# Stick-breaking weights as differences, and the softmax division and the sum of product halves moved to the gates

## Chip, core and metric

The program runs on one core of a Trainium2 chip. The metric is the device time of one execution in microseconds (us). The core's engines are TensorE (PE, with its weight loads listed as PEld), VectorE (DVE), ScalarE (ACT), GpSimd (POOL) and SyncE (SP). In this kernel SP issues every DMA.

## The reference, cut to what matters

One layer of a hybrid encoder, for a prompt of 1024 frames and a sample of 32 frames with shared weights. All is float32. The features are 1024; `w_in` gives eight groups of 512 columns, and A and B have 8 heads of 64 each.

```python
u = rmsnorm(h, g_pre) @ w_in
qa, ka, va, ga, qb, kb, vb, gb = split(u)

# A: band attention
s = einsum('bqhd,bkhd->bhqk', q, k) * SCALE + bias_table[:, clip(k_pos - q_pos)]
oa = softmax(where(ok, s, -1e30)) @ v        # 640 keys at most for each 128 queries

# B: stick breaking, k_pos < q_pos
z = einsum('bqhd,bkhd->bhqk', q, k) * SCALE
log_1m = where(causal, log_sigmoid(-z), 0)
after = cumsum(log_1m, reverse=True) - log_1m
ob = where(causal, exp(log_sigmoid(z) + after), 0) @ v

y = concat(oa * silu(ga), ob * silu(gb)) @ w_out
h = h + rmsnorm(y, g_post)
h = h + sigmoid(h @ w_ple_gate) * (p @ w_ple)
```

The sigmoid products of B are a running product from the right: with s' = sigmoid(-z) and C(k) the product of s' over the keys from k on, the weight of key k is sigmoid(z_k) · C(k+1), which equals C(k+1) − C(k), since sigmoid(z) = 1 − sigmoid(−z).

## The kernel before, in words

**Accuracy and matmuls.** Every float32 product is made of three matmuls with operands split in a high and a low part (`wh`, `wl`, `hnh`, `hnl`, `wTh`, `wTl`). A projection chunk is 352 columns (3 chunks cover the 1056 frames) and takes 24 matmuls.

**Stages.** First x is normalised, turned and split (to about 60 us of the profiled span), while the first weights come in. Then attention runs for four pairs of heads of A and four of B, in turn (A0, B0, A1, B1 and so on), woven with the projections q, k and v of the next pair (60 to 480 us). The last pair, B3, is woven with the eight gate products gA0 to gB3 (482 to 606). Then come the product of p with `w_ple`, and the output projection and gate as Strassen-like block products (to about 797 us).

**Attention.** `attention` (L778) makes three kinds of units for each head. `scores(i)` (L813) makes the scores of query block i (128 queries) in PSUM tiles `SA` or `SB`, and the weights from them in two SBUF tiles, `om` and `be` (the names of the two rings, L514). For A, DVE adds the bias and takes the maximum, negates it, ACT makes the exponential with its sum, DVE takes the reciprocal, POOL multiplies. For B, DVE adds the mask, ACT makes two sigmoids, of −s in `om` and of s in `be`; DVE scans the products over `om` from the right, and POOL multiplies `be` by it. `weights_t(i)` (L860) turns the weights: PE transposes into PSUM `ptw`, ACT copies the high part to `wTh`, DVE subtracts for the low part `wTl`. For A's blocks 4 and 6 (`ROUND`, L31) it goes another way, here called the swap path: DVE transposes in squares of 32, one DMA writes them to DRAM (`swapA`), four DMAs read them back turned into `be`, ACT casts `wTh` and DVE subtracts `wTl`. `values(g)` (L910) multiplies four query blocks by the value operand (`v2`), into a PSUM tile `PV` of 128 partitions, whose two halves of 64 belong to high and low parts of the values. ACT copies one half, DVE adds the other, and a DMA stores 64 rows in `o_dr`.

**Gates.** In `col_steps` (L712) a gate chunk of 352 columns gets its `o_dr` part by a DMA that is issued with its first matmuls (tiles `ogg`, at L730). At its end ACT makes a sigmoid, DVE multiplies the sum by it, POOL multiplies by `ogg`, and a DMA stores to `og_dr` (tiles `sgg`, L741 to L746).

**What sets the order.** All calls are recorded (`Recorder.add`, L308, so that L450 stands for every line in the profile) and `order()` (L372) writes a fixed order for each engine. It is a list scheduler: it gives each operation a cost and the time at which its inputs are there, and among the ready ones takes attention first on PE and the earliest recorded on other engines. Its times carry margins ahead of PE (400 ns) and behind a DMA (2000 ns). In this order each engine runs strictly. In the built program each DMA on SP waits, besides its own inputs, until the DMA eight places before it has landed.

**At the start** SP loads the norm's weights, p, x's tiles 0 to 2, the first weights of k and q, x's tile 3, then masks, tiles 5 and 6, `wr_vA` in two halves around tile 4, and tile 7. x's tiles are `om` in the profile, but tiles 3 and 4, `x`. For each tile ACT squares it with a sum (`be<-om`), POOL makes `rs`, DVE scales it to `be`, PE turns it (`ptx`) and ACT and DVE split it (`hnh`, `hnl`). POOL splits the weights `wr` of k, q and v in between; those of vA go to the tile `wTl`.

Of the kernel before, what the change touches and what calls it, by code (L numbers as in the profile page):

```python
# [8 lines left out]
F32 = mybir.dt.float32  # L9
# [21 lines left out]
ROUND = {"A": ((4,),(6,)), "B": ()}  # L31
# [127 lines left out]
class Segments:  # L159


    def __init__(self, buf, start, step, n):
        self.buf, self.start, self.step, self.n = buf, start, step, n
        self.shape = [buf.shape[0], n, P]
        self.box = (buf.box[0], (start, start + (n - 1) * step + P))

    def get(self):
        base = self.buf.get()[:, self.start:self.start + P]
        return bass.AP(tensor=base.tensor, offset=base.offset, ap=[base.ap[0], [self.step, self.n], [1, P]])
# [83 lines left out]

class Engine:
# [9 lines left out]
class Recorder:  # L264
# [43 lines left out]
    def add(self, eng, what, args, kw):  # L308
        writes, reads = [], []
        method = what[1] if isinstance(what, tuple) else ""  # L310
        for i, a in enumerate(args):
            if isinstance(a, (View, Raw, Segments)):
                (writes if i == 0 or (method == "tensor_tensor_reduce" and i == 7) else reads).append(a)
        for k, a in kw.items():
            if isinstance(a, (View, Raw, Segments)):
                (writes if k in ("out", "accum_out") else reads).append(a)
        o = self.node(eng, what, args, kw, set())
        for mine, write in ((reads, False), (writes, True)):
            for v in mine:
                b = v.buf  # L320
                hit = False
                for other, box, wrote in b.uses:
                    if other is not o and (write or wrote) and all(p < y and x < q for (p, q), (x, y) in zip(v.box, box)):
# [6 lines left out]
                b.uses.append((o, v.box, write))  # L330
        o.busy, o.late = self.cost(eng, method, args, kw, writes, reads)
        o.shared = eng == "POOL"
        if eng == "DVE":
            sbuf = [v for v in reads if isinstance(v, (View, Segments)) and not v.buf.psum and v.free() > 4]
# [3 lines left out]
    def cost(eng, method, args, kw, writes, reads):  # L338
# [3 lines left out]
        psum = any(isinstance(v, (View, Segments)) and v.buf.psum for v in reads)  # L342
# [97 lines left out]
    def emit(self, tc):  # L440
        ops = self.order()
        with tc.manual_schedule():
            for o in ops:
# [3 lines left out]
                args = [a.get() if isinstance(a, (View, Raw, Segments)) else a for a in o.args]  # L447
                kw = {k: a.get() if isinstance(a, (View, Raw, Segments)) else a for k, a in o.kw.items()}
# [7 lines left out]
def stream_step(  # L456
# [22 lines left out]
    o_dr = [scratch([P, T], f"o_dr{n}") for n in range(8)]  # L479
# [34 lines left out]
    ring0, ring1 = Arena(rec, at, "om", 3076), Arena(rec, at, "be", 3384)  # L514
    ringh, ringl = (Arena(rec, at, x, 33 * P, F32R) for x in ("wTh", "wTl"))
# [10 lines left out]
    NAMES = ["qA", "kA", "vA", "gA", "qB", "kB", "vB", "gB"]  # L526

# [14 lines left out]
    def ensure(j):  # L542
# [6 lines left out]
        if j == 2:  # L549
            pair = [ringl.tile([P, 2, 4, P], f"w{x}_{kind}{p}") for x in "hl"]  # L550
# [14 lines left out]
    def load_x(t):  # L565
        n = min(P, T - t * P)
        if t == 3:
            x34.append(at.tile([P, ringh.cols], F32, tag="wTh", name="x34")[:, 0:2 * D].rearrange("p (a c) -> p a c", a=2))
# [37 lines left out]
    def bias_rows():  # L606

        rb = ring0.tile([8, 257], "rb")
        dma(rb, rel_bias[0])
        R = ring1.tile([8, 768], "R")  # L610
# [101 lines left out]
    def col_steps(j):  # L712
# [7 lines left out]
        def mms(c, part):  # L720
# [9 lines left out]
            if k == "g" and part == 0:  # L730
                box["og"] = at2.tile([P, CH], F32, tag="bias", name=f"og{kind}{p}_{c}", bufs=2)
                dma(box["og"], o_dr[n][:, cs])
# [8 lines left out]
            if k == "g":  # L741
# [3 lines left out]
                nc.gpsimd.tensor_tensor(sg, sg, box["og"], ALU.mult)  # L745
                dma(og_dr[n, :, cs], sg)  # L746
            elif k == "q":
                nc.scalar.activation(box["st"][:, cs], acc, AF.Copy, scale=SCALE)
# [28 lines left out]

    def attention(ab, p, h):  # L778
# [5 lines left out]
        def begin():  # L784
            if ab == "A":
                bias = at2.tile([P, 640], F32, tag="bias", name=f"bias{nm}", bufs=2)
                dma(bias, bias_src(2 * p + h, P, 0, 640))
                nc.gpsimd.memset(bias[0:HD, 0:HD], NEG)
                nc.gpsimd.memset(bias[HD:P, 576:640], NEG)
# [4 lines left out]

        together = {i: g for g in ROUND[ab] for i in g}
        whole, done_with = {}, []
# [4 lines left out]
        def rooms(i):  # L801

            more = ab == "B"
            g = together.get(i, (i,))
            if g not in whole:
                n = sum(cost(x) for x in g) * P
                whole[g] = ring0.tile([P, n + more * len(g)], f"om{nm}_{i}"), ring1.tile([P, n], f"be{nm}_{i}")
            k, n = g.index(i), cost(i) * P
            a = sum(cost(x) for x in g[:k]) * P
            w0, w1 = whole[g]  # L810
            return w0[:, a + more * k:a + more * k + n + more], w1[:, a:a + n]

        def scores(i):  # L813
# [5 lines left out]
            w0, w1 = rooms(i)  # L819
# [8 lines left out]
            if ab == "B":  # L828
# [3 lines left out]
                nc.gpsimd.memset(w0[:, n:n + 1], 1.0)  # L832
                for a, b, s in pieces:
                    nc.scalar.activation(w0[:, a:b], s, AF.Sigmoid, scale=-1.0)
                for a, b, s in pieces:
                    nc.scalar.activation(w1[:, a:b], s, AF.Sigmoid)
                for a, b, s in reversed(pieces):
                    rev = w0[:, a + 1:b + 1][:, ::-1]
                    nc.vector.tensor_tensor_scan(rev, rev, s, 1.0 if b == n else w0[:, b + 1:b + 2], ALU.mult, ALU.bypass)
                nc.gpsimd.tensor_tensor(w1[:, 0:n], w1[:, 0:n], w0[:, 1:n + 1], ALU.mult)  # L840
            else:
                m = small.tile([P, 4], F32, tag="stat", name=f"stat{nm}_{i}", bufs=6)
                for j, (a, b, s) in enumerate(pieces):
                    nc.vector.tensor_tensor_reduce(
                        w0[:, a:b], s, box["bias"][:, n - b:n - a][:, ::-1], 1.0,
                        -3e38 if j == 0 else m[:, j - 1:j], ALU.add, ALU.max, m[:, j:j + 1])
# [7 lines left out]
        wT = {}  # L854
# [5 lines left out]
        def weights_t(i):  # L860
            g = i // 4
            step, size = LAID[ab, g]
            if g not in wT:
                wT[g] = [x.tile([P, size * P], f"{x.name}{nm}_{g}") for x in (ringh, ringl)]
            b0 = lo_block(i)
            w0, w1 = state.pop(i)
            n = i + 1 - b0
            at_ = ((i - 4 * g) * step + b0) * P
            hi, lo = (x[:, at_:at_ + n * P] for x in wT[g])
            if i in together:  # L870

                group = together[i]
                done_with.append((i, hi, lo))
                if i != group[-1]:
                    return
                w0, w1 = whole[group]
                m = sum(cost(x) for x in group)
                first = {x: sum(cost(y) for y in group[:k]) for k, x in enumerate(group)}
                squares = w0[:, 0:m * P].rearrange("p (c b q) -> p b c q", c=4, q=32)
                for x, _, _ in done_with:  # L880
                    y = slice(first[x], first[x] + cost(x))
                    nc.vector.transpose(squares[:, y], w1[:, y.start * P:y.stop * P])
                dr = scratch([P, m * P], f"swap{nm}_{i}")
                dma(dr, w0[:, 0:m * P])
                for c in range(4):
                    x = dr[:, c * m * 32:(c + 1) * m * 32].rearrange("(g k) x -> k g x", k=32)
                    dma(w1[32 * c:32 * c + 32].rearrange("k (g x) -> k g x", g=4), x)
                turned = w1.rearrange("p (g b q) -> p g b q", g=4, q=32)
                for x, hi, lo in done_with:
                    src = turned[:, :, first[x]:first[x] + cost(x), :]  # L890
                    hi, lo = (y.rearrange("p (b g q) -> p g b q", g=4, q=32) for y in (hi, lo))
                    nc.scalar.copy(hi, src)
                    nc.vector.tensor_tensor(lo, src, f(hi), ALU.subtract)
                done_with.clear()
                return
            for b in range(0, n, 4):
                m = min(4, n - b)
                pt = psum("T", f"ptw{nm}_{i}_{b}")
                for x in range(m):
                    nc.tensor.transpose(pt[:, x * P:(x + 1) * P], w1[:, (b + x) * P:(b + x + 1) * P], ident)  # L900
                c = slice(b * P, (b + m) * P)
                nc.scalar.copy(hi[:, c], pt[:, 0:m * P])
                nc.vector.tensor_tensor(lo[:, c], pt[:, 0:m * P], f(hi[:, c]), ALU.subtract)
# [6 lines left out]
        def values(g):  # L910
# [6 lines left out]
            for n, (b, j, half) in enumerate(todo):  # L917
                c = reach(g, b)
                step = LAID[ab, g][0]
                w = Segments(wT[g][half], c.start * step + b * P, step * P, (c.stop - c.start) // P)  # L920
# [26 lines left out]
    def sample_attention(ab, gi):  # L947
# [44 lines left out]
        def scores():  # L992
# [6 lines left out]
            w0 = ring0.tile([P, NK + 1], "w0" + nm)  # L999
            w1 = ring1.tile([P, NK], "w1" + nm)  # L1000
            if ab == "B":
                new = pieces[1][2][:, NK // 2 - NS:NK // 2]
                nc.vector.tensor_tensor(new, new, masks, ALU.add)
                nc.gpsimd.memset(w0[:, NK:NK + 1], 1.0)
                for a0, b0, s in pieces:
                    nc.scalar.activation(w0[:, a0:b0], s, AF.Sigmoid, scale=-1.0)
# [844 lines left out]
```

## Time and profile before

| | us |
|---|---|
| three runs | 805.87, 806.26, 806.33 |
| median | 806.26 |
| span of the profiled execution | 802.6 |

The profiled execution has no time of its own beside its span; the median lies 3.66 us above the span. The core's mean granted TensorE clock is 0.999. The page lists, for each engine, its busy time, its share of the span and its instructions. A wait is idle time of an engine just before an instruction, put down to the semaphore event that came last. A row "PE a <- DVE b" reads: PE waited, ahead of an instruction that writes a, for DVE's b. Tile names stand without their buffer numbers, and names that differ by pair are shortened (`wr_kA`).

### The profile page before, as it was taken

Reading aid. Unit: us, or ns where it says so; the run is one execution under the profiler, and the core shown is the slowest. Engines: PE = TensorE matmul, PEld = TensorE weight load, DVE = VectorE, ACT = ScalarE, POOL = GpSimd, SP = SyncE. Lnnn points to the kernel's source line nnn. Section 1 sums busy time; section 2 is a strip of 40 time slices with the busy share of each in tenths; the row PEclk is TensorE's granted clock in tenths of the full one; section 3 lists DMA queues with packets and bytes.
Section 4 is the critical chain, followed back from the end, with each engine's and each line's share of the span. In section 5 each row is a group of like instructions: output and inputs, shape, how many; then the busy total and the mean of one; then the engine's idle time right before and its main releaser. Section 6 shows DMA issues by size and latency. Waiting matters only on the chain.

```text
span 802.6 us, 14554 instructions
## 1 busy us (share of the span) xinstructions
PE 792.0 (99%) x4734; PEld 731.4 (91%) x4734; DVE 565.7 (70%) x1129; ACT 539.5 (67%) x1163; POOL 469.5 (58%) x554
## 2 busy tenths in 40 slices
PE   9999999999999999999999999999999999999997
PEld 7899999999999999999999899999998877888786
DVE  7627878777787888776787586854554786587655
ACT  6636787786586777776787577644437868876741
POOL 6625867795686866635473265554553448599613
PEclk9999999999999999999999999999999999999999
DMA  9419986538876565833325656344389957769634
GB/s 293 135 46 285 236 230 186 153 112 254 220 229 198 145 184 158 208 103 102 92 60 141 146 158 205 99 149 138 105 277 300 288 174 242 236 197 345 215 117 131
DMA packets 147390, 146.32 MB, mean 182 GB/s; under 512 B 37409, under 2 KB 109257, under 8 KB 147314
## 3 DMA queue, kind: packets, MB, share of 16 engines
q1 hardware_dynamic: 147314, 145.39, 61.3%
q8 instruction: 38, 0.62, 0.3%
q14 instruction: 38, 0.31, 0.1%
HBM read 90.78 MB, written 46.16 MB: 171 GB/s over the span
## 4 chain that ended last, share of the span: by engine, by line
PE 89%; DVE 3%; DMA 2%; POOL 2%; ACT 1%; issue 1%; SPq 1%; POOLq 0%; DVEq 0%; ACTq 0%
PE mm_gB L450 6%; PE mm_gA L450 6%; PE mm_kB L450 6%; PE mm_qB L450 6%; PE mm_qA L450 5%; PE mm_kA L450 5%; PE mm_vB L450 4%; PE PVB L450 4%; PE mm_vA L450 4%; PE SB L450 4%; PE ptwB L450 4%; PE SA L450 3%; PE PVA L450 3%; PE g0P L450 2%; PE g1P L450 2%; PE o1P L450 2%
## 5 line engine op out<-in xcount | busy, mean ns | idle before, releaser
L450 POOL TENSOR_TENSOR be<-be,om 128x512 f32<-128x512 f32 (+8 forms) x66 | 82.9, 1260 | 77.8 <-DVE om L450 43.9
L450 DVE TENSOR_TENSOR_SCAN om<-om,SB 128x384 f32<-128x384 f32 (+5 forms) x96 | 92.6, 968 | 21.9 <-ACT be L450 11.7
L450 POOL TENSOR_SCALAR be<-be,statA 128x640 f32<-128x640 f32 (+3 forms) x64 | 44.4, 698 | 44.4 <-DVE statA L450 35.8
L450 DVE TENSOR_TENSOR wTl<-ptwB,wTh 128x512 fp32r<-128x512 f32 (+3 forms) x96 | 50.8, 546 | 13.8 <-ACT wTh L450 12.4
L450 ACT ACTIVATE om<-SB 128x384 f32<-128x384 f32 (+5 forms) x96 | 47.4, 499 | 19.0 <-DVE SB L450 14.2
L450 ACT CAST wTh<-ptwB 128x512 fp32r<-128x512 f32 (+3 forms) x96 | 44.6, 483 | 14.5 <-PE ptwB L450 10.5
L450 ACT ACTIVATE be<-om,statA 128x640 f32<-128x640 f32 (+3 forms) x64 | 44.6, 698 | 11.2 <-DVE statA L450 9.6
L450 ACT ACTIVATE be<-SB 128x384 f32<-128x384 f32 (+5 forms) x96 | 46.8, 498 | 6.8 <-DVE om L450 6.3
L450 PE MATMUL ptwB<-ident,be 128*128 128x128 f32 x288 | 44.0, 273 | 0.1
L450 PEld LDWEIGHTS ptwB<-ident,be 128*128 128x128 f32 x288 | 34.9, 140 | 2.2 <-PE mm_vA L450 0.4
L450 DVE CUSTOM_DVE_ANT_0 om<-SA,biasA 128x320 f32<-128x320 f32 (+2 forms) x64 | 30.7, 480 | 5.3 <-PE SA L450 4.9
L450 PE MATMUL SB<-kdB,LB 128*128 128x384 f32 (+5 forms) x96 | 34.0, 357 | 0.3 <-DVE om L450 0.3
L450 ACT CAST wTh<-ptwA 128x512 fp32r<-128x512 f32 (+2 forms) x64 | 26.0, 429 | 12.0 <-PE ptwA L450 11.4
L450 DVE TENSOR_TENSOR wTl<-ptwA,wTh 128x512 fp32r<-128x512 f32 (+2 forms) x64 | 29.7, 482 | 4.9 <-ACT wTh L450 4.0
L450 PE MATMUL SB<-klB,LB 128*128 128x384 f32 (+5 forms) x96 | 32.9, 347 | 0.0
L450 PE MATMUL SA<-kdA,LA 128*128 128x320 f32 (+2 forms) x96 | 30.0, 319 | 1.1 <-DVE LA L450 0.8
L450 PE MATMUL SA<-klA,LA 128*128 128x320 f32 (+2 forms) x96 | 29.8, 319 | 0.0
L450 POOL TENSOR_TENSOR gB<-gB,gB 128x256 f32<-128x256 f32 x32 | 26.6, 848 | 0.7 <-DMA gB<-in_w_ple_gate_dram 0.4
L450 PE MATMUL ptwA<-ident,be 128*128 128x128 f32 x160 | 26.5, 274 | 0.0
L450 DVE TENSOR_TENSOR SB<-SB,maskb 128x128 f32<-128x128 f32 x64 | 18.0, 292 | 9.9 <-PE SB L450 8.0
L450 POOL TENSOR_TENSOR oB<-oB,oB 128x256 f32<-128x256 f32 x32 | 23.6, 754 | 1.4 <-DMA oB<-in_w_out_dram 1.3
L450 POOL TENSOR_TENSOR h<-h,x 128x512 f32<-128x512 f32 (+1 forms) x18 | 23.0, 1295 | 0.8 <-DVE h L450 0.8
(706 smaller groups left out, 2668.3 us busy)
## 6 DMA issues: line engine op xcount, KB each, us to landing
swapA<-om SPq DMA_DIRECT2D x16, 320.0 KB, 3.5
be<-swapA SPq DMA_DIRECT2D x64, 80.0 KB, 2.9
oB<-in_w_out_dram SPq DMA_DIRECT2D x16, 256.0 KB, 3.9
sum_dro<-oB SPq DMA_DIRECT2D x16, 256.0 KB, 2.9
gB<-in_w_ple_gate_dram SPq DMA_DIRECT2D x16, 256.0 KB, 3.7
sum_drg<-gB SPq DMA_DIRECT2D x16, 256.0 KB, 3.2
x<-in_x_prompt_dram SPq DMA_DIRECT2D x16, 256.0 KB, 4.1
h_dr<-h SPq DMA_DIRECT2D x8, 512.0 KB, 3.6
```

Of the source, the lines that this page charges most:

```text
L450: getattr(getattr(tc.nc, o.what[0]), o.what[1])(*args, **kw)
```

## The change

**B's weights.** One sigmoid is made, of −s, in one tile `w` with a column of ones behind it. DVE scans in place, and POOL subtracts: the column behind minus the column itself.

**A's weights.** q is scaled by −SCALE, the table of `rel_bias` is negated and the mask is +1e30, so that the scores are kept negated; the minimum takes the place of the maximum and goes into the exponential as it is (`scale=-1.0`). The weights stay undivided. Their sums are kept in a tile of 8 columns; after block 7 DVE takes one reciprocal, and a DMA stores 1024 numbers in `rs_dr`.

**Turned weights.** `wTh` and `wTl` are now rings of 33 slots laid as 4 groups of 32 columns, with a dependency for each block. The moving operand of a value matmul is read in runs of 32 columns. On the swap path the four DMAs land in the low part itself, ACT casts the high part from it, and POOL (`LOE`) instead of DVE subtracts in place.

**Values and gates.** ACT copies all 128 partitions of `PV`, and two DMAs store the halves in two tensors. The gate loads both halves, and for A the reciprocals by two DMAs that repeat a row over 64 partitions; DVE adds the halves, POOL multiplies by the reciprocals (A) and then by the gate. The columns of the sample frames, which have only one half and are divided already, get zeros and ones in the second tensor and in `rs_dr` by nine DMAs in `fixed_columns`, called after `bias_rows` at the start. `AHEAD_OF` comes out empty, so `late_gate` isn't called.

```diff
+    def fixed_columns():
+        x = small.tile([P, 2, NS], F32, tag="fixed", name="fixed")
+        nc.gpsimd.memset(x[:, 0], 0.0)
+        nc.gpsimd.memset(x[:, 1], 1.0)
+        for n in range(8):
+            dma(o_dr[n][1][:, SEQ:T], x[:, 0])
+        dma(rs_dr[:, SEQ:T], x[0:8, 1])
...
+    def outputs(ab, p, c):
+        cs = slice(c * CH, (c + 1) * CH)
+        x = at2.tile([P, 3, CH], F32, tag="stg", name=f"ol{ab}{p}_{c}", bufs=3)
+        for part in range(2):
+            dma(x[:, part], o_dr[sidx(ab, p)][part][:, cs])
+        if ab == "A":
+            for h in range(2):
+                row = rs_dr.real[2 * p + h:2 * p + h + 1, cs]
+                dma(x[h * HD:(h + 1) * HD, 2], Raw(rs_dr, bass.AP(tensor=row.tensor, offset=row.offset, ap=[[0, HD], [1, CH]])))
+        return x
+
+    def finish_gate(ab, sg, x):
+        GATE_ENG[0].tensor_tensor(x[:, 0], x[:, 0], x[:, 1], ALU.add)
+        if ab == "A":
+            GATE_ENG[1].tensor_tensor(x[:, 0], x[:, 0], x[:, 2], ALU.mult)
+        nc.gpsimd.tensor_tensor(sg, sg, x[:, 0], ALU.mult)
...
                 for a, b, s in pieces:
-                    nc.scalar.activation(w0[:, a:b], s, AF.Sigmoid, scale=-1.0)
-                for a, b, s in pieces:
-                    nc.scalar.activation(w1[:, a:b], s, AF.Sigmoid)
+                    nc.scalar.activation(w[:, a:b], s, AF.Sigmoid, scale=-1.0)
                 for a, b, s in reversed(pieces):
-                    rev = w0[:, a + 1:b + 1][:, ::-1]
-                    nc.vector.tensor_tensor_scan(rev, rev, s, 1.0 if b == n else w0[:, b + 1:b + 2], ALU.mult, ALU.bypass)
-                nc.gpsimd.tensor_tensor(w1[:, 0:n], w1[:, 0:n], w0[:, 1:n + 1], ALU.mult)
+                    rev = w[:, a:b][:, ::-1]
+                    nc.vector.tensor_tensor_scan(rev, rev, s, 1.0 if b == n else w[:, b:b + 1], ALU.mult, ALU.bypass)
+                nc.gpsimd.tensor_tensor(w[:, 0:n], w[:, 1:n + 1], w[:, 0:n], ALU.subtract)
...
-                nc.vector.tensor_scalar(m[:, 2:3], m[:, last:last + 1], -1.0, None, ALU.mult)
-                nc.scalar.activation(w1[:, 0:n], w0[:, 0:n], AF.Exp, bias=m[:, 2:3], accum_out=m[:, 3:4])
-                nc.vector.reciprocal(m[:, 3:4], m[:, 3:4])
-                nc.gpsimd.tensor_scalar(w1[:, 0:n], w1[:, 0:n], m[:, 3:4], 1.0, ALU.mult, ALU.mult)
-            state[i] = w0, w1
+                sums = box["sums"]
+                nc.scalar.activation(w[:, 0:n], w[:, 0:n], AF.Exp, bias=m[:, last:last + 1], scale=-1.0, accum_out=sums[:, i:i + 1])
+                if i == 7:
+                    nc.vector.reciprocal(sums, sums)
+                    dma(rs_dr[2 * p + h, 0:SEQ].rearrange("(i q) -> q i", q=P), sums)
+            state[i] = w
...
+            if i in ROUND[ab]:
+                x = ring1.tile([P, n * P], f"x{nm}_{i}")
+                nc.vector.transpose(x.rearrange("p (c b q) -> p b c q", c=4, q=32), w[:, 0:n * P])
+                dr = scratch([P, n * P], f"swap{nm}_{i}")
+                dma(dr, x)
+                landed = f(lo).rearrange("p g s q -> p g (s q)")
                 for c in range(4):
...
+                    dma(landed[32 * c:32 * c + 32], dr[:, c * n * 32:(c + 1) * n * 32].rearrange("(g k) x -> k g x", k=32))
+                nc.scalar.copy(hi, f(lo))
+                (nc.gpsimd if LOE == "P" else nc.vector).tensor_tensor(lo, f(lo), f(hi), ALU.subtract)
                 return
...
-            nc.scalar.copy(ot[r], acc[o])
-            nc.vector.tensor_tensor(ot[r], acc[r], ot[r], ALU.add)
-            dma(o_dr[sidx(ab, p)][r, 4 * g * P:4 * (g + 1) * P], ot[r])
+            nc.scalar.copy(ot, acc)
+            for part, rows in enumerate((r, o)):
+                dma(o_dr[sidx(ab, p)][part][r, 4 * g * P:4 * (g + 1) * P], ot[rows])
```

More of the change, by code (lines that the diff above doesn't have):

```diff
@@ L341, in cost @@
         n = out.free() if isinstance(out, View) else 1
-        psum = any(isinstance(v, (View, Segments)) and v.buf.psum for v in reads)
+        psum = any(isinstance(v, (View, Span)) and v.buf.psum for v in reads)
         if eng == "PE":
@@ L513, in stream_step @@
     opnd = [at0, at]
-    ring0, ring1 = Arena(rec, at, "om", 3076), Arena(rec, at, "be", 3384)
-    ringh, ringl = (Arena(rec, at, x, 33 * P, F32R) for x in ("wTh", "wTl"))
+    ring0, ring1 = Arena(rec, at, "om", 3076), Arena(rec, at, "be", 3304)
+    ringh, ringl = (Ring(rec, at, x, SLOTS) for x in ("wTh", "wTl"))
+    early = at.tile([P, SLOTS * P], F32R, tag="wTl", name="early")
     def rstd_of(ms, name, n):
@@ L729, in mms @@
             cs = slice(c * CH, (c + 1) * CH)
-            if k == "g" and part == 0:
-                box["og"] = at2.tile([P, CH], F32, tag="bias", name=f"og{kind}{p}_{c}", bufs=2)
-                dma(box["og"], o_dr[n][:, cs])
+            if k == "g" and part == 0 and (kind, p) not in AHEAD_OF:
+                box["og"] = outputs(ab, p, c)
             W = loaded[j]
@@ L801, in rooms @@
         def rooms(i):
[L803 to L811, printed above, removed]
+            n = cost(i) * P
+            return ring0.tile([P, n + (ab == "B")], f"w{nm}_{i}")
         def scores(i):
@@ L863, in weights_t @@
             if g not in wT:
-                wT[g] = [x.tile([P, size * P], f"{x.name}{nm}_{g}") for x in (ringh, ringl)]
+                wT[g] = ringh.base(size), ringl.base(size)
             b0 = lo_block(i)
-            w0, w1 = state.pop(i)
+            w = state.pop(i)
             n = i + 1 - b0
[L868 to L884, printed above, removed]
-                for c in range(4):
[L886 to L894, printed above, removed]
@@ L1184, in stream_step @@
     pairs = [("A", 0), ("B", 0), ("A", 1), ("B", 1), ("A", 2), ("B", 2), ("A", 3), ("B", 3)]
-    gates = [("gA", p) for p in range(4)] + [("gB", p) for p in range(4)]
-    share = {7: 8}
+    share = SHARE
+    AHEAD_OF = set()
     order = []
@@ L1193, in stream_step @@
             order += [(k + ab, p) for k in "kqv"]
-        for _ in range(share.get(n, 0)):
-            order.append(gates.pop(0))
+        for kind, q in share.get(n, ()):
+            order.append((kind, q))
+            if n < {"gA0": 3, "gA1": 3, "gB0": 4, "gB1": 4}.get(f"{kind}{q}", 7):
+                AHEAD_OF.add((kind, q))
         span.append((a, len(order)))
@@ L1384, in stream_step @@
     bias_rows()
+    fixed_columns()
     for h in range(4):
```

163 lines of the change are left out of this document (107 added, 56 removed).

## The prediction

> **What bounds the kernel now.** I read the page's first and fourth parts, then the busy time by stage (columns: window, its length, busy time of PE, PEld, DVE, ACT and POOL with instruction counts, PE's granted clock, DMA share, GB/s), and last the waits of PE (total, times, longest).
>
> ```profile
> span 802.6 us, 14554 instructions
> PE 792.0 (99%) x4734; PEld 731.4 (91%) x4734; DVE 565.7 (70%) x1129; ACT 539.5 (67%) x1163; POOL 469.5 (58%) x554
> PE 89%; DVE 3%; DMA 2%; POOL 2%; ACT 1%; issue 1%; SPq 1%; POOLq 0%; DVEq 0%; ACTq 0%
> ```
>
> ```profile
> 0.00:60.00 60.00, 56.97 (x335) 51.94 (x336) 33.09 (x53) 31.90 (x63) 28.39 (x54) 1.00 0.50 157
> 60.00:480.00 420.00, 417.59 (x2715) 403.29 (x2714) 326.23 (x741) 307.64 (x682) 262.16 (x325) 1.00 0.62 172
> 480.00:606.00 126.00, 126.00 (x811) 123.59 (x810) 76.17 (x128) 66.30 (x151) 68.43 (x71) 1.00 0.53 163
> 606.00:803.00 197.00, 191.49 (x879) 152.60 (x877) 130.26 (x208) 133.61 (x270) 110.50 (x105) 1.00 0.69 224
> ```
>
> ```profile
> PE idle L450 <- DVE newh L450: 1.3, 1, 1.3
> PE ptx L450 <- DVE be L450: 0.9, 1, 0.9
> PE SA L450 <- DVE LA L450: 0.8, 1, 0.8
> PE ptx L450 <- DVE hnl L450: 0.8, 2, 0.6
> PE mm_vB L450 <- ACT wh_vB L450: 0.4, 1, 0.4
> PE SB L450 <- DVE om L450: 0.3, 1, 0.3
> PE PVA L450 <- ACT wTh L450: 0.2, 1, 0.2
> PE SA L450 <- DVE statA L450: 0.2, 1, 0.2
> ```
>
> PE is busy for 99% of the span and makes 89% of the chain that ended last, at the full clock in every stage. In the attention stage (60 to 480 us) it is idle for 420.00 − 417.59 = 2.4 us, in the gate stage (480 to 606) for nothing. The rest (606 to 803) idles 5.5 us, in the output projection and the tail, which this change doesn't edit. So all that lighter DVE, ACT and POOL can give is these 2.4 us, and waits too short to be seen, since matmuls are pipelined and their ends are modelled:
>
> ```profile
> 44.72 4.08 PE mm_qA L450 x24
> 48.80 3.88 PE mm_vA L450 x24
> ```
>
> The chain shows 24 equal matmuls in 3.88 us (0.162 us each) and in 4.08 us, and no wait row names that 0.2 us. I allow 2 us of such hidden waits for the lower end of the range and none in the sum.
>
> **What is removed.** Of the costliest groups (busy us, mean ns | idle before):
>
> ```profile
> L450 ACT ACTIVATE be<-SB 128x384 f32<-128x384 f32 (+5 forms) x96 | 46.8, 498 | 6.8 <-DVE om L450 6.3
> L450 POOL TENSOR_SCALAR be<-be,statA 128x640 f32<-128x640 f32 (+3 forms) x64 | 44.4, 698 | 44.4 <-DVE statA L450 35.8
> L450 DVE TENSOR_TENSOR otA<-PVA,otA 64x512 f32<-64x512 f32 x16 | 11.0, 687 | 8.3 <-ACT otA L450 8.1
> L450 DVE TENSOR_TENSOR wTl<-be,wTh 128x640 fp32r<-128x640 f32 x16 | 18.1, 1131 | 4.6 <-ACT wTh L450 4.2
> ```
>
> ACT loses the second sigmoid, 46.8 us of 307.6 + 66.3. POOL loses the normalise, 44.4 us. DVE loses 32 additions of halves (16 for A at 687 ns, 16 for B taken alike: 22 us), the 16 subtractions of swapped blocks (18.1 us), and 64 negates and 56 reciprocals of one column, which I leave out: 40 us of 326.2 + 76.2. The matmuls keep their number (4,736 in both built programs) and sizes, so none of this shortens the bound engine; it can only take away PE's waits on the others. Of the 2.4 us in the attention stage, 0.8 is for LA, an operand of the first scores that the change leaves alone. The other 1.6 us (mm_vB on ACT, SB on the scan, PVA on wTh, SA on statA, and what no row names) stand behind ACT's and DVE's queues, which become 10 to 13% emptier. I take 1.4 of the 1.6: **−1.4 us** (bounds 0 and −1.6, or −3.6 with hidden waits).
>
> **Startup.** One edit is there, nine DMAs of fixed columns, which SP issues between x's tile 3 and tile 5, ahead of the masks. In this order SP, ACT, POOL, DVE and PE stand around them now:
>
> ```profile
> SPq L450 <- DMA x<-in_x_prompt_dram: 0.8, 1, 0.8
> ```
>
> ```profile
> 12.74 2.52 SPq L450 DMA_DIRECT2D masks<-maskb  x4
> 15.37 0.99 SPq L450 DMA_DIRECT2D om<-in_x_prompt_dram  x2
> 17.68 0.33 SPq L450 DMA_DIRECT2D x<-in_x_prompt_dram  x1
> 21.35 1.08 ACT L450 ACTIVATE be<-om 128x1024 f32<-128x1024 f32 x1
> 23.17 0.61 POOL L450 CAST wTl<-wr_vA 128x512 fp32r<-128x512 f32 x1
> 25.24 0.22 POOL L450 TENSOR_SCALAR rs<-ms 128x1 f32<-128x1 f32 x1
> 26.77 0.22 POOL L450 TENSOR_SCALAR rs<-ms 128x1 f32<-128x1 f32 x1
> 27.68 1.41 DVE L450 SCALAR_TENSOR_TENSOR be<-x,rs,gpre 128x512 f32<-128x512 f32 x2
> 28.57 0.63 PE L450 MATMUL ptx<-ident,be 128*128 128x128 f32 x4 [0.87 <-DVE be L450]
> ```
>
> ```profile
> om<-in_x_prompt_dram SPq DMA_DIRECT2D x6, 512.0 KB, 5.1
> ```
>
> A DMA waits for the one eight places before it. So far tile 4's load (17.68) is the one that waits for tile 3's; with the fixed columns it is tile 5's, which leaves at 17.7 instead of 15.4 and by the median lands at 22.8. ACT's squares (1.08, and 0.2 to read the sum) end at 24.1. POOL now splits half of vA's weights (23.17 to 25.24), makes tile 5's rs (to about 26.1), casts the other half, makes tile 3's rs (26.77), from which DVE scales tile 3 (27.68), for which PE waits 0.87 us at ptx. In the new program POOL's order has tile 5's rs first, then the two halves, then tile 3's rs: the same work, but nothing of it starts before 24.1 where it now runs from 23.17. So tile 3 and PE's wait come 0.9 us later; if tile 5 lands in 4 us, nothing is lost. The load of vA's first half goes from 16.45 behind tile 6 and three masks (0.63 each by the row) to about 21, close to the time when POOL wants it. I take **+0.7 us** (bounds 0 and +3, the latter if these loads come 2 us later still).
>
> **What is added or moved in attention.** All of it is off PE, and what hides it is PE's own queue. The 16 swapped blocks of A land in the low part, and the subtraction goes from DVE to POOL. Once per head a reciprocal is made and 1,024 words of 4 bytes are stored; in SP's order the store stands ahead of a block's four loads back.
>
> ```profile
> L450 POOL TENSOR_TENSOR wl_qA<-wr_qA,wh_qA 128x512 fp32r<-128x512 f32 x8 | 10.2, 1295 | 1.2 <-ACT wh_qA L450 1.1
> out_dram<-ktB SPq DMA_DIRECT2D x16, 128.0 KB, 3.9
> ```
>
> ```profile
> 101.23 0.83 DVE L450 TENSOR_TENSOR wTl<-be,wTh 128x640 fp32r<-128x640 f32 x1 [1.60 <-ACT wTh L450]
> 102.53 0.74 PE L450 MATMUL PVA<-wTl,v2A 128*128 128x512 f32 x4
> ```
>
> By the nearest row POOL takes 1,295 × 640/512 = 1.6 us against DVE's 1.1. The store isn't in this trace: the nearest row, kt's stores of 1,024 short runs, landed in 3.9 us, so it holds the loads back by 0 to 3.9. The path grows by 0.5 to 4.4 us, and it had 0.5 us to spare here (102.53 − 102.06). But PE's order moves too: in the eight A heads, from the last score of block 6 to the first value matmul of the second half, there stand 154 to 227 instructions now and 204 to 281 in the new order, 30 to 105 more in each head. At 0.162 us that is 5 to 17 us more cover (an estimate, some being shorter transposes). I take **0**; with that cover gone it would be up to 3.9 us in each of 8 heads.
>
> The value matmuls read their weights in runs of 32 columns instead of 128. In 135,168 columns (1,056 times 128) that is 3,168 more jumps.
>
> ```profile
> L450 PE MATMUL PVB<-wTl,v2B 128*128 128x512 f32 x48 | 16.1, 412 | 0.0
> L450 PE MATMUL PVB<-wTh,v2B 128*128 128x512 f32 x48 | 15.4, 398 | 0.0
> L450 PE MATMUL SB<-klB,LB 128*128 128x512 f32 x24 | 9.7, 404 | 0.0
> ```
>
> PVB reads 4 runs of 128, SB one of 512: 405 ns on the mean against 404. Three jumps cost at most this 1 ns, so 1,056 times three 1 us; by the slower PVB row 8 ns, or 8.4 us. I take **0**, since the two PVB rows differ by more than their mean does from SB's. The Trainium skill ("Advanced Engine Details and Errata", section "Memory Cachelines") asks of SBUF at least two hits on each 16-byte line, and says that of PSUM any non-contiguous pattern "significantly slows down matmuls". By the first, runs of 32 words cost nothing, and the trace agrees for runs of 128; the second, taken to hold for these operands as well, would be the third rival below.
>
> The halves of the value product are stored apart (32 more stores), and nothing waits for them before the gates.
>
> **Gates.** DVE gains 24 additions of 128x352, POOL 12 products, SP 24 loads of halves and 24 of reciprocals.
>
> ```profile
> oggA<-o_dr SPq DMA_DIRECT2D x12, 176.0 KB, 3.0
> ```
>
> At no more than wl_qA's 1.3 us each, the products are 16 us on a POOL busy 68.4 of 126 and the additions 31 us on a DVE busy 76.2, both beside PE. The loads (3.0 us) go out with a chunk's first matmuls, 3.9 us before its last, so the additions are done by then, and behind the last gate stands one POOL product, as before. **0** (bounds 0 and +1, POOL's product after the last gate coming one operation later).
>
> **The sum**: 802.6 − 1.4 + 0.7 = 801.9 us of span. The median, 806.26, lies 3.66 us above the profiled span; with the same 3.66 the forecast is **805.6 us**.
>
> **The rivals.**
> Faster (chance 0.26): the hidden waits go with the visible ones (−3.6 instead of −1.4), and tile 5 lands in 4 us, so that startup costs nothing: 806.26 − 3.6 = 802.7. For it speaks the 4.08 beside 3.88 us; against it, that this example lies in a stage where the change removes nothing.
> Slower by the swap path (0.13): at the first value matmul that reads a swapped block PE waits for POOL's subtraction, which queues behind one further POOL operation (1.3 us) or whose loads stand behind the short-run store (3.9). It decides once the path grows by more than the 5 us of cover that the tightest heads gain. One such store's delay in one head and one POOL operation in half of them is 3.9 + 4 × 1.3 = 9 us at the most; I price it at half, 805.6 + 4.5 = 810.1. Against it stands the longer distance on PE.
> Slower by the runs of 32 (0.10): between 1 and 8.4 us on the sum, 806.6 to 814, over all value matmuls, with no wait to be seen.
> Slower by startup (0.12): +3 instead of +0.7, and 807.9 with the rest of the sum.
>
> **How the numbers follow.** The forecast keeps 0.39, and its own range is 804 to 807. A measurement of this kernel can tell 0.2%, 1.6 us, from no change: under 804.65 is faster, over 807.87 slower. Faster: 0.26 and 0.10 of the forecast's, 0.36. Slower: 0.13, and most of the other two, 0.18: 0.31. The same: 0.33. The range goes from 801.8 (the faster rival with 1 us more) to 810.1 (the swap path as priced), which leaves out the upper half of the runs' price and swap waits in all heads.
>
> **What would show it.** In the waits of PE: ptx on be grown to about 1.6 us (startup right), gone or beyond 3 us (wrong); fewer rows and under 1.5 us of idle time between 60 and 480 us; no PVA or PEld row that waits for POOL's wTl. PVB's mean beside SB's within 5 ns means that the runs cost nothing. I am wrong if the new order itself brings waits on ACT or DVE, which the sum holds at nothing, or if the gate stage shows PE idle at all.

## The result, and the profile after

The changed kernel takes 869.53 us (median of 4 runs, 868.44 to 870.99) against 806.19: a ratio of 1.0775, 95% interval 1.0745 to 1.0804. The forecast was 805.6, with a range from 801.8 to 810.1. The profiled execution spans 867.4 us.

The page's first lines and its chain that ended last, of the kernel after:

```profile
span 867.4 us, 14262 instructions
PE 812.1 (94%) x4734; PEld 742.4 (86%) x4734; DVE 538.8 (62%) x984; ACT 500.2 (58%) x1063; POOL 455.9 (53%) x520
PEclk9999988999969899999999999899999999999999
PE 73%; DMA 14%; SPq 3%; DVE 3%; POOL 3%; ACT 2%; issue 1%; POOLq 0%; ACTq 0%; DVEq 0%
```

DVE, ACT and POOL are lighter, as the change has it. PE ran the same 4,734 recorded matmuls, idle for 867.4 − 812.1 = 55.3 us where it was idle for 10.6, and busy for 20 us more, at a granted clock that is no longer full everywhere. DMA's share of the chain went from 2% to 14%. By stage, and by what PE waited for:

```profile
0.00:60.00 60.00, 54.57 (x315) 49.56 (x316) 32.44 (x53) 29.64 (x60) 25.46 (x53) 0.97 0.53 157
60.00:550.00 490.00, 446.01 (x2784) 424.19 (x2783) 294.19 (x594) 285.06 (x625) 243.57 (x287) 0.95 0.69 159
550.00:676.00 126.00, 125.93 (x791) 121.61 (x789) 82.84 (x133) 56.46 (x120) 77.33 (x77) 1.00 0.73 217
676.00:868.00 192.00, 185.61 (x849) 147.03 (x848) 129.32 (x205) 128.99 (x261) 109.50 (x104) 0.99 0.68 222
```

```profile
PE PVA L492 <- ACT wTh L492: 8.5, 2, 8.2
PE ptwA L492 <- ACT ktB L492: 7.8, 1, 7.8
PE SB L492 <- DVE om L492: 6.6, 2, 6.3
PE ptvB L492 <- ACT stvB L492: 6.1, 1, 6.1
PE mm_vB L492 <- ACT wh_vB L492: 3.7, 1, 3.7
PE ptx L492 <- DVE be L492: 2.3, 1, 2.3
```

Most of the loss lies in the attention stage. The row from 60 to 550 us also holds the first 14 us of the gates: the first gate product starts at 536.1 us, where it started at 480.7 before, 55 us later. From there the gates take 133 us instead of 125, and what follows them takes as long as before (198 against 197). The largest waits name five different tiles, made by ACT and DVE, which have less to do than before. That points to a common cause behind them, and the longest DMAs on the chain show where to seek it:

```profile
121.88 12.19 DMA wTl<-swapA
224.46 12.74 DMA rs_dr<-sumsA
367.67 13.73 DMA rs_dr<-sumsA
400.44 12.13 DMA rs_dr<-sumsA
```

The three stores of 1,024 reciprocals, 4 KB each, that stand on the chain take 12 to 14 us from issue to landing. Next comes SP's queue around the second of the eight such stores (start, length, DMA, count; rows in between are left out), then a wait of SP's over the whole run, and the windows around the second store:

```profile
118.60 0.38 SPq L492 DMA_DIRECT2D rs_dr<-sumsA  x1
119.82 0.54 SPq L492 DMA_DIRECT2D sum_dro<-oB  x1
121.09 0.75 SPq L492 DMA_DIRECT2D wr_vA<-in_w_in_dram  x1
121.88 0.67 SPq L492 DMA_DIRECT2D wTl<-swapA  x1
122.66 0.48 SPq L492 DMA_DIRECT2D klB<-klB  x1
131.13 0.33 SPq L492 DMA_DIRECT2D oB<-in_w_out_dram  x1
```

```profile
SPq L492 <- DMA sum_dro<-oB: 9.0, 2, 7.9
```

```profile
122.60:131.10 8.50, 4.11 (x20) 3.82 (x19) 2.13 (x3) 1.36 (x3) 1.34 (x2) 0.88 0.80 51
131.10:138.00 6.90, 3.06 (x10) 2.96 (x11) 2.01 (x2) 2.12 (x4) 5.43 (x6) 0.53 0.71 200
```

SP issues nothing for 8 us after the DMA at 122.66. The next one, at 131.13, loads `oB`, and the row's longest wait (7.9 us) is there, for the store `sum_dro<-oB`. That store was issued 1.2 us behind the reciprocals and so took some 11 us to land, where the median of such stores is 3.4. For the reciprocals themselves SP waits 12.2 us in the whole run (4 times, 5.3 at the longest). In the 8.5 us from 122.6 the DMA engines are busy for 0.80 of the time and move 51 GB/s, where the stage's mean is 159. A load of a swapped block issued behind the store (80 KB, 3.6 us by its median) lands after 12.19 us, and PE waits 8.2 us for what ACT makes of it; the clock falls to 0.53.

### The profile page after: what moved, and what is told of

It reads as the page before. It is cut to its first block, busy times and chain, and to the rows that moved or that the text cites. A ratio compares the mean times of both kernels' runs of the same rounds, so it can differ in the third digit from the quotient of the medians.

```text
span 867.4 us, 14262 instructions
## 1 busy us (share of the span) xinstructions
PE 812.1 (94%) x4734; PEld 742.4 (86%) x4734; DVE 538.8 (62%) x984; ACT 500.2 (58%) x1063; POOL 455.9 (53%) x520
## 4 chain that ended last, share of the span: by engine, by line
PE 73%; DMA 14%; SPq 3%; DVE 3%; POOL 3%; ACT 2%; issue 1%; POOLq 0%; ACTq 0%; DVEq 0%
PE mm_gB L492 5%; PE mm_qA L492 5%; PE mm_vA L492 5%; PE mm_gA L492 5%; DMA rs_dr<-sumsA 4%; DMA wTl<-swapA 4%; PE mm_kA L492 4%; PE PVB L492 4%; PE mm_kB L492 4%; SPq L492 3%; PE ptwB L492 3%; PE SB L492 3%; PE SA L492 3%; PE PVA L492 3%; PE o1P L492 2%; PE g0P L492 2%
## 5 line engine op out<-in xcount | busy, mean ns | idle before, releaser
L492 POOL TENSOR_TENSOR om<-om 128x256 f32<-128x256 f32 (+8 forms) x66 | 77.2, 1176 | 48.1 <-DVE om L492 42.4
L492 ACT ACTIVATE om<-SB 128x384 f32<-128x384 f32 (+5 forms) x96 | 44.6, 496 | 25.7 <-DVE SB L492 19.2
L492 ACT ACTIVATE om<-om,statA 128x640 f32<-128x640 f32 (+3 forms) x64 | 44.5, 697 | 13.4 <-DVE statA L492 12.8
L492 PE MATMUL ptwB<-ident,om 128*128 128x128 f32 x288 | 45.1, 276 | 0.9 <-DVE wTl L492 0.6
L492 PEld LDWEIGHTS ptwB<-ident,om 128*128 128x128 f32 x288 | 35.5, 142 | 3.5 <-POOL om L492 0.8
L492 DVE CUSTOM_DVE_ANT_0 om<-SA,biasA 128x320 f32<-128x320 f32 (+3 forms) x64 | 30.0, 483 | 13.0 <-PE SA L492 8.4
L492 PE MATMUL ptwA<-ident,om 128*128 128x128 f32 x160 | 26.7, 275 | 9.4 <-ACT ktB L492 7.8
L492 POOL TENSOR_TENSOR wTl<-wTl,wTh 128x640 fp32r<-128x640 f32 x16 | 24.9, 1561 | 19.9 <-ACT wTh L492 19.7
L492 PEld LDWEIGHTS ptwA<-ident,om 128*128 128x128 f32 x160 | 19.9, 141 | 10.5 <-ACT ktB L492 8.1
L492 PE MATMUL PVA<-wTh,v2A 128*128 128x512 f32 (+1 forms) x96 | 20.2, 335 | 8.7 <-ACT wTh L492 8.5
```

Source lines behind the costliest of these rows:

```text
L492: getattr(getattr(tc.nc, o.what[0]), o.what[1])(*args, **kw)
```

## The experiments

**Theory one**: the store of single words holds up every DMA behind it. **Theory two**, from the prediction's rivals: the reads in runs of 32, or the swapped blocks through POOL. Four kernels, the first with the very order of the changed one. Its stores write the same bytes in runs of 32; it leaves out the order in which the gates read the reciprocals:

```diff
-dma(rs_dr[2 * p + h, 0:SEQ].rearrange("(i q) -> q i", q=P), sums)
+dma(rs_dr[2 * p + h, 0:SEQ].rearrange("(q i) -> q i", i=8), sums)
```

> The changed kernel, in which each of the 8 stores of A's reciprocals writes 128 runs of 8 numbers instead of 1024 single numbers; same bytes, same order of every instruction (so A's queries are divided by each other's sums, which this kernel leaves wrong). Theory one: the 1024 single words hold the DMA queues for some 12 us at each of the 8 stores, and PE runs out of work behind late loads. It expects 803 to 809 us, the stores landing in under 4 us, and PE idle under 6 us between 60 and 480 us. Theory two: the reads in runs of 32 columns slow the value matmuls, or the swapped blocks are late by POOL. It expects 855 to 870 us.

828.65 us (ratio 1.0268, interval 1.0241 to 1.0296). The store's row is now

```profile
rs_dr<-sumsA SPq DMA_DIRECT2D x8, 4.0 KB, 3.9
```

One access pattern in 8 DMAs is worth 869.5 − 828.7 = 41 us. It is not the whole loss: both theories missed. The next kernel turns the reciprocals first:

```diff
+                    nc.vector.reciprocal(tt[:, 0:8], sums)
+                    nc.vector.transpose(tt[:, 32:64], tt[:, 0:32])
+                    rows = rs_dr[2 * p + h, 0:SEQ].rearrange("(i c q) -> c i q", c=4, q=32)
+                    for c in range(4):
+                        dma(rows[c], tt[32 * c:32 * c + 8, 32:64])
```

> The changed kernel computing all of it: the reciprocals of a head are turned on DVE in squares of 32 and stored by 4 DMAs in runs of 128 bytes. Theory one expects 803 to 809 us, within 3 us of the kernel with runs of 32 bytes. Theory two expects 855 to 870 us.

819.89 us (1.0153, 1.0129 to 1.0178): 50 us of the loss are gone, 14 are left. Then the suspected store alone, in the kernel before:

```diff
+                if i in (5, 7):
+                    dma(rs_dr[2 * p + h, 256 * (i - 5):256 * (i - 5) + 512].rearrange("(i q) -> q i", q=P), m)
```

> The kernel before, which computes all of its outputs, with two more stores in each head of A, after blocks 5 and 7: 512 single numbers each from the statistics tile to a scratch tensor that nobody reads. Theory one expects 6 us to landing for each of the 16 stores, and the program slower by 20 to 60 us (826 to 866). Theory two, by which such a store is as cheap as others, expects 806 to 809 us.

891.44 us (1.1021, 1.098 to 1.1061): 85 us for 16 stores of 2 KB that nobody reads, more than theory one expected; one of them stands on the chain, and it landed after 9.71 us. And in runs of 4 numbers (`"(q i) -> q i", i=4`):

> The same two more stores in the kernel before, with 128 runs of 4 numbers each instead of 512 single ones, in the same order of every instruction. Theory one and theory two both expect 805 to 809 us; if it is slower than that, 16 more stores of any kind cost time here by delaying what is behind them in SP's order.

811.41 us (1.0061, 1.0037 to 1.0086), landing in 2.7 us at the median. The two kernels run every instruction in the same order, so 80 of the 85 us come from the pattern of the store alone, and theory one is shown, for single words. Even the runs of 4 numbers cost 5 us; whether as stores in the queue or as a new order stays open.

**The other 14 us.** Theory two's parts, and the startup, one by one. Fixed columns stored in the fifth pair's stage:

> The kernel with the turned store (819.9 us), in which the nine DMAs of fixed columns are issued in the fifth pair's stage instead of at the start. If they hold up x's tile 5 as the prediction has it, PE's wait of 2.4 us at ptx falls back to about 0.9 and the kernel to 818 to 819 us. If the start is late for another reason it stays at 819 to 821.

822.68 us (815.14 to 823.95; 1.0173, 1.0142 to 1.0204), no gain in the time; PE waits 2.1 us at ptx (in two pieces) instead of 2.4. In the profiled executions PE does 330 matmuls in the first 60 us instead of 325 (335 before). The spread of this kernel is wider than the effect, so the time doesn't tell. `LOE = "D"`:

> The kernel with the turned store, in which DVE instead of POOL subtracts in the 16 swapped blocks. If POOL's subtraction is what makes the rest of the loss (the prediction's swap rival), 806 to 814 us. If the rest lies in the order as such and in the start, 816 to 823 us.

815.64 us (1.0088, 1.0062 to 1.0114): between the two, 4 us less.

B's weights alone, on the kernel before:

> The kernel before with B's weights alone changed (in the prompt's heads): one sigmoid, the scan in place, POOL's subtraction of neighbours. If the lighter ACT takes waits from PE, 803 to 805 us; if it gains nothing that PE can use, 805 to 807; if a new order costs time by itself, more than 808.

818.21 us (1.0127, 1.0101 to 1.0153). The gates' part alone:

> The kernel before with the halves of the value product stored apart, loaded by the gates and added there by DVE; the columns of zeros are stored late, A's weights are divided as before. If the 32 more stores, 24 more loads and 24 additions lie beside PE, 805 to 807 us; if they crowd the gate stage, PE idles between 480 and 606 us and the kernel takes 808 to 815.

816.42 us (1.0098, 1.0075 to 1.0122), though PE idles nowhere in the gate stage. Each part, with nothing added on PE, costs 9 to 12 us. **Theory three**: any change gives the list scheduler another order, and the order before happens to suit. So the same kernels were redrawn, that is given another order by one constant of the planner (the list scheduler):

> The kernel before with nothing changed but the planner's margin ahead of PE, 380 ns instead of 400, so that the same instructions come in another order. If the order before is one that happens to suit, and any new draw costs time, 810 to 820 us, with new waits of PE between 190 and 300 us. If orders are alike, 805 to 808 us, and the loss of the parts tried alone (11 and 9 us) is their own.

> The kernel before with the planner's time of a semaphore at 70 ns instead of 60: a second new draw of the same instructions. As for the first: 810 to 820 us if a new draw costs, 805 to 808 if not.

> The kernel with the turned store (819.9 us) with the margin of 380 ns. If the rest of its loss is the draw, it takes anything from 808 to 822 us, as the redrawn kernel before does; if the rest is the change's own, it stays within 3 us of 820 while the redrawn kernel before stays at 806.

> The kernel with the turned store, with the semaphore time of 70 ns: as for the margin of 380, 808 to 822 us if it is the draw, 817 to 823 if the change's own.

The kernel before: 810.72 (1.0045, 1.002 to 1.0069) and 809.76 us (1.0033, 1.0012 to 1.0055), so these two new draws cost 3 to 4 us, at or just under the lower end of what was expected. The waits expected between 190 and 300 us came in the second only (PE idles there for 0.1 and 5.0 us). The kernel with the turned store: 824.98 us, above both ranges, and 821.04 us. Its three draws lie at 822.0 us on the mean, those of the kernel before at 808.9, and the lowest of the one is 9 us above the highest of the other. Theory three explains a part, and 9 to 13 us are the change's own, as far as three orders of each tell. Of the loss of the two parts tried alone, 5 to 8 us are beyond these draws; each had one draw, and the cause stays open.

**Theory four** came from the stage of pair A1, which holds the sample's attention (PE's last vB and first kA rows, SP's load of the weights of kA between them, and the sample's value product PVsA). The kernel before, then the one with the turned store:

```profile
224.54 0.28 PE L450 MATMUL PVsA<-Vh0sA,whsA 128*128 128x256 f32 x1
238.62 1.21 PE L450 MATMUL mm_vB<-hnl,wh_vB 128*128 128x352 f32 x6
239.67 1.46 PE L450 MATMUL mm_kA<-hnh,wh_kA 128*128 128x352 f32 x8
...
229.49 0.93 SPq L450 DMA_DIRECT2D wr_kA<-in_w_in_dram  x2
```

```profile
239.30 0.70 PE L492 MATMUL mm_vB<-hnl,wh_vB 128*128 128x352 f32 x3
241.42 0.80 PE L492 MATMUL PVA<-wTl,v2A 128*128 128x512 f32 x4
242.90 0.39 PE L492 MATMUL PVsA<-Vh0sA,whsA 128*128 128x256 f32 x1
253.06 0.74 PE L492 MATMUL mm_kA<-hnh,wh_kA 128*128 128x352 f32 x3 [0.93 <-ACT wh_kA L492]
...
247.72 1.05 SPq L492 DMA_DIRECT2D wr_kA<-in_w_in_dram  x2
```

Before, the next projection follows the last one at once. With the change PE has no projection for 13 us (240.00 to 253.06). In the 13.4 us from 239.7 it does 62 matmuls, nearly all of attention, and is busy for 10.32 us; the next kernel, in the 13.4 us before its first mm_kA, does 90 and is never idle. The code suggests why: there is one `PV` tile in PSUM (`PS_BUFS`), so PVsA comes after A's second value product; PVsA's operands lie in the four `wr` buffers, so the next weights (`wr_kA`) can be loaded only behind it. And the second value product is late because the loads of a swapped block land in the ring of low parts, where an older block's value product must have been done first. That is undone alone in the next kernel, which lands them in the tile that held the turned squares:

```diff
-                landed = f(lo).rearrange("p g s q -> p g (s q)")
+                landed = x.rearrange("p (g s q) -> p g s q", g=4, q=32)
...
-                nc.scalar.copy(hi, f(lo))
+                nc.scalar.copy(hi, landed)
```

> The kernel with the turned store (819.9 us), in which the four loads of a swapped block land in the tile that held the turned squares, not in the low part itself; ACT casts and POOL subtracts from there, as DVE did before. If the loads into the ring of low parts wait for the value product that still reads that place, and so make the second value product, the sample's product behind it and the next weights' loads late, this gives back 6 to 11 us: 809 to 814 us, the first mm_kA of the third pair starting within 1 us of the last mm_vB of the stage. If not, 817 to 822.

810.79 us (1.0046, 1.0027 to 1.0066), 9.1 us less than the first draw of the turned store, and the rows are back in their places:

```profile
229.37 0.28 PE L492 MATMUL PVsA<-Vh0sA,whsA 128*128 128x256 f32 x1
242.56 1.46 PE L492 MATMUL mm_vB<-hnl,wh_vB 128*128 128x352 f32 x8
243.85 0.49 PE L492 MATMUL mm_kA<-hnh,wh_kA 128*128 128x352 f32 x2
...
233.47 1.37 SPq L492 DMA_DIRECT2D wr_kA<-in_w_in_dram  x2
```

The time without a projection tells the same in the other kernels. With the stores of single words out of the way, it is 11 to 15 us in all five in which the loads land in the ring and POOL subtracts, and nothing in all five in which they land elsewhere (the four below included). In the kernel with DVE's subtraction it is 6.4 us (241.33 to 247.76). So POOL's subtraction seems to make about half of it, but only where the loads land in the ring; with the other place it is gone while POOL still subtracts.

With DVE's subtraction and late fixed columns besides, in four draws:

> The same landing place, with DVE subtracting and the fixed columns stored late: everything found so far set back but the change's arithmetic. If these are the causes, it takes what a new draw of the kernel before takes, 806 to 811 us; more than 813 leaves a further cause.

> The kernel of the run before in a new draw (semaphore time 70 ns): 804 to 812 us as the draws of the kernel before spread, and over 813 if a cause is left.

> The kernel with the other landing place, DVE's subtraction and late fixed columns in a third draw (margin 380 ns): 804 to 814 us, since the first two draws gave 813.6 and 805.2 and the kernel before's three gave 806.4 to 810.7.

> The same in a fourth draw (semaphore time 80 ns): 804 to 814 us. If the change's arithmetic, with its faults set back, is worth something beyond the draw, the mean of its four draws lies under the 808.9 us of the kernel before's three; if not, at or over it.

813.62 (1.0078, 1.005 to 1.0105), 805.18 (0.9974, 0.9954 to 0.9994), 810.35 (1.006, 1.0043 to 1.0077) and 811.33 us (1.007, 1.0055 to 1.0085). The first is above the 813 that by its expectation leaves a further cause; 2.5 us of it are, in its profile, the wait at g0P of the last section, and the rest stays open. The mean is 810.1; the kernel before's three draws (806.2, 810.7, 809.8) have 808.9. With its faults set back, the change's arithmetic is worth nothing that these draws can tell. The second draw is the only kernel of the study that beats the kernel before, by 0.26%; with three slower draws of the same instructions beside it, that is put down to the draw.

## Why the prediction was wrong, point by point

**What bounds the kernel, and how little there was to win: right.** By the rows of the stages, DVE's busy time in attention and gates fell from 402.4 to 377.0 us (6%, where 10 was predicted) and ACT's from 373.9 to 341.5 us (9%, where 13 was), and no kernel of the study gained more than 1.2 us.

**Removal, −1.4 us: not borne out.** The waits counted on do not go with lighter engines; each draw of the order makes its own. From 60 us to the first gate product PE idles for 2.4, 6.2 and 6.5 us in the three draws of the kernel before, and for 2.4 to 7.1 us in the four draws with the faults set back. B's part alone, which takes work from ACT but also keeps its weights in the ring of `om` until they are turned, came out 12 us slower in its one draw, with PE's largest wait at the sample's scores (4.8 us for QsA).

**Startup, +0.7 us: right in sign, too small.** PE's wait at ptx grew from 0.9 to 2.3 us (1.6 was predicted), but that sign is a poor one: with no fixed columns at all it is 0.9 us in the kernel before with runs of 4 numbers and 2.1 in the one with single words, which run in the same order. The work done in the first 60 us tells more. PE does 308 to 327 matmuls there in the seven kernels with the nine DMAs at the start, and 330 to 335 in the twelve without them; it idles for 5.5 and 3.8 us on the mean. By these means they cost some 1.8 us. Tile 5 was not the late one: its rs ran at 23.97, as worked out. What the prediction had only in its bound came true, the load of vA's weights. POOL's rows of the kernel after:

```profile
23.97 0.22 POOL L492 TENSOR_SCALAR rs<-ms 128x1 f32<-128x1 f32 x1
25.87 0.61 POOL L492 CAST early<-wr_vA 128x512 fp32r<-128x512 f32 x1 [1.01 <-DMA wr_vA<-in_w_in_dram]
28.65 0.61 POOL L492 CAST early<-wr_vA 128x512 fp32r<-128x512 f32 x1 [0.78 <-DMA wr_vA<-in_w_in_dram]
29.35 0.22 POOL L492 TENSOR_SCALAR rs<-ms 128x1 f32<-128x1 f32 x1
```

Both halves land late, and tile 3's rs behind them comes 2.6 us later than before (26.77).

**The swap path, 0 us: this step failed, twice.** First in the price: "The store isn't in this trace: the nearest row, kt's stores of 1,024 short runs, landed in 3.9 us, so it holds the loads back by 0 to 3.9." Those runs are of 128 bytes, these of 4, and the store landed after 12 to 14. It was also charged to four loads alone, where other DMAs behind it were late too, weights included; so the rival's 810.1 was nearly as far off as the forecast (59 us against 64). That is some 41 to 50 us of the 63 (by the run with 32-byte runs and by the turned store).

Second in the cover: "PE's order moves too [...] 30 to 105 more in each head." The added instructions ahead of the second value product were read as cover. By the code, and by what the other landing place gave back, they were the delay itself: the planner had seen the loads wait for their place in the ring, and let PE use up the stage's projections meanwhile. Nothing was left for the time until the next weights came. The kernel with the other landing place puts this at 9 us. What the rival had, PE waiting for POOL's subtraction at a value product, is a row of only 0.6 us in the changed kernel; a subtraction took 1.56 us there, as estimated.

**The runs of 32, 0 us: right.** The kernel after:

```profile
L492 PE MATMUL PVB<-wTl,v2B 128*128 128x512 f32 x48 | 15.9, 413 | 0.0
L492 PE MATMUL PVB<-wTh,v2B 128*128 128x512 f32 x48 | 15.5, 404 | 0.0
L492 PE MATMUL SB<-klB,LB 128*128 128x512 f32 x24 | 10.0, 418 | 0.0
```

PVB's mean, 408.5 ns, lies 3.5 ns above the 405 of the kernel before and under that of SB, which is read without jumps. At 3.5 ns for 512 columns the 135,168 columns make 0.9 us at the most. So the first of the two rules cited there held, as far as these rows show, and the second doesn't reach these operands, which lie in SBUF.

**Gates, 0 us: right for the gates' own work.** In the changed kernel PE idles for 0.07 us in the 126 from 550 us on, but for 6.2 us in the whole gate stage (536.1 to 669.5), which the prediction named as a sign of being wrong. Of this, 6.1 us are the wait at `ptvB` above. It stands behind the last store of reciprocals (issued at 527.50) and a load of the gates' weights that landed after 11.63 us. With the turned store PE idles for nothing between the first gate product and the last.

**A new order costs nothing: wrong**, by 3 to 4 us for the kernel before. The prediction named this as what could make it wrong and gave it no price.

**The last step, 3.66 us from span to median, isn't fixed.** In the executions on record whose span is known, the time lies 1.7 to 2.6 us above the span of the same execution (1.8 at the median). So the profiled execution of the kernel before was one of its quicker ones. (The lower end of the range, 802.7 − 1, is 801.7 rather than 801.8.) Neither matters beside 63 us.

## What to carry to other kernels

Count the runs of a DMA and their length, not its bytes alone, and price it as delay of everything behind it in the queue; where no row of the trace has runs that short, the price is open upwards. Before a buffer is merged with the one that a transfer lands in, ask what must have left that place first, and who waits behind. In a kernel with a planned order, redraw the order of the unchanged kernel once or twice before a change of a per cent is put down to the change.

## What the runs showed of the hardware

**Single words.** Three stores of 1,024 words of 4 bytes took 12.1 to 13.7 us to land; in 32-byte runs the median of eight was 3.9.

**A DVE instruction can be kept out for long by POOL.** In the kernel with runs of 32 bytes, and then in the changed kernel, whose order is the same on both engines:

```profile
748.35 2.57 POOL L492 TENSOR_TENSOR ug<-ug,s 128x512 f32<-128x512 f32 x2
749.64 8.08 DVE L492 TENSOR_TENSOR gT<-raw,gT 128x512 fp32r<-128x512 f32 x1
750.85 1.32 POOL L492 TENSOR_TENSOR gT<-raw,gT 128x512 fp32r<-128x512 f32 x1
752.10 1.32 POOL L492 TENSOR_TENSOR gB<-raw,gB 128x512 fp32r<-128x512 f32 x1
753.35 1.32 POOL L492 TENSOR_TENSOR cc2P<-cc2P,hh 128x512 f32<-128x512 f32 x1
754.60 2.58 POOL L492 TENSOR_TENSOR gB<-raw,gB 128x512 fp32r<-128x512 f32 x2
```

```profile
792.04 2.54 POOL L492 TENSOR_TENSOR ug<-ug,s 128x512 f32<-128x512 f32 x2
793.34 1.80 DVE L492 TENSOR_TENSOR gT<-raw,gT 128x512 fp32r<-128x512 f32 x1
794.55 1.74 POOL L492 TENSOR_TENSOR gT<-raw,gT 128x512 fp32r<-128x512 f32 x1
```

In the second, DVE gets in behind POOL's ug, and POOL's next instruction is longer for it (1.74 against 1.32). In the first, DVE's instruction, which reads two SBUF operands, lasts 8.08 us, until POOL has run five more instructions without a gap, and PE then waits 2.5 us at g0P. The instructions and their order are the same, and what decides between the two was not settled. The long instruction (8.06 to 8.09 us), with a wait of 2.4 to 2.5 us at g0P, stands in the profiles of seven kernels: the one with runs of 32 bytes, the turned store in two of its draws, the ones with DVE's subtraction and with the other landing place, and two of the last four draws. It stands in no profile of the kernel before or its two new draws. So it makes some 2.5 us of the differences between these profiles. The Trainium skill, "SBUF — State Buffer", section "SBUF: two separate sides", says that the two engines share an exclusive lock which the first to start holds for a whole instruction. The rows agree that they exclude each other, and add that the loser may miss five turns.
